# The order in which scores, values and transpositions are written inside the attention units of a hybrid backbone step

## The chip, the cores and the metric

The kernel runs on one core of a Trainium2 chip. The metric is the device time of one execution in microseconds (us); lower is better. The matrix engine (TensorE, PE in the profile) multiplies into PSUM banks; VectorE (DVE), ScalarE (ACT) and GpSimd (POOL) work beside it; SyncE (SP) issues most of the transfers.

## The reference

One layer of a diffusion backbone for 1024 latent tokens and 128 context tokens (1152 in all, D_MODEL 1024): adaLN-modulated RMSNorm, one input projection, a Fourier token mixer and windowed grouped-query attention beside each other, a gated merge, an output projection and a squared-ReLU MLP. What matters here is the attention: 16 query heads in 4 key/value groups, head dimension 64, blocks of 128 queries, a window of 128 tokens to either side, all cached context keys besides, and a learned sink logit per head.

```python
def attend_block(qb, k_all, v_all, sink, mask):
    scores = jnp.einsum('btkgd,blkd->bkgtl', qb, k_all,
                        preferred_element_type=jnp.float32) * (HEAD_DIM ** -0.5)
    if mask is not None:
        scores = jnp.where(mask[None, None, None], scores, NEG_INF)
    sink_col = jnp.broadcast_to(sink.astype(jnp.float32).reshape(N_KV_HEADS, Q_PER_KV)[None, :, :, None, None],
                                scores.shape[:-1] + (1,))
    p = jax.nn.softmax(jnp.concatenate([scores, sink_col], axis=-1), axis=-1)[..., :-1]
    return jnp.einsum('bkgtl,blkd->btkgd', p.astype(v_all.dtype), v_all)
```

The modulation vectors of the layer, `silu(c) @ w_ada + b_ada`, are also computed while attention runs.

## The kernel before, in words

All products are made in float32 precision from a high and a low part of each operand, so an operand x is split into a rounded copy (ScalarE) and the difference (`sub`, L142, VectorE).

The attention stage runs 36 units, one for each pair of key/value group g (0 to 3) and block i of 128 queries (0 to 8; block 8 is the context block). `KWIN` (L43) gives the number nb of 128-key blocks that block i reads: 3 for i = 0 and i = 7, 1 for i = 8, else 4. A unit has up to three kinds of attention steps on TensorE, and each step belongs to a unit of its own age:

- **S**, a score: `score_head(u, h)` (L1008), one for each of the group's four heads of the present unit. Two matmuls (L1024, L1025) into an "s" bank (two of them), one VectorE reduction that adds the mask and takes the maximum (L1026), the exponential on ScalarE (L1038) and, after every second head, a reciprocal on VectorE (L1048) and two multiplications on GpSimd (L1050) that normalise the probabilities "pt".
- **T**, a transposition: `out_t(u, b)` (L1061), one for each key block b of the unit before. Four transposes (L1064) into a "ptp" bank (three of them), the high part "ph" on ScalarE (L1067) and the low part "pl" on VectorE (`sub`, L142).
- **V**, a value step: `out_v(u, b)` (L1071), one for each key block of the unit before that. Two matmuls (L1079, L1080) accumulate in the single "o" bank. After the last block ScalarE copies (L1089) and VectorE adds (L1093, tile "at") the halves, and two stores (L1098) bring the result to `att_d`.

Two more kinds of PE work use the same banks. `put_k` (L1116, called **K** here) transposes key blocks for the scores into a "ptp" bank; `next_keys` (L1361) calls it after the units i = 0, 4 and 7 of a group. `mod_fold` (L272, called **F**, the fold) finishes a block of modulation vectors: one small matmul (L278) into an "s" bank and four small VectorE adds (L282, tile "mods") which free it. It was called once after every unit from s = 3 on, if at least two blocks waited (from s = 30 on, at least one). Ten folds were made in the stage.

The written order of TensorE's instructions holds in this stage (`tc.manual_schedule`, L986); the other engines' queues are ordered by the planner from its own estimate of the time line. Between the steps stand fillers, three matmuls each: pieces of the gate projections, of the next group's queries (whose rotary embedding costs VectorE the pieces L865 to L883) and of the Fourier branch. `unit_order` (L1372) writes the list of a unit's steps with a `None` wherever a filler may go, and the main loop (L1392 to L1408) spreads the fillers of the stage over these places in proportion to the unit's key blocks. After each step `tick` (L899) advances a counter, and work that was put off with `defer` (L893) is issued when the counter reaches it: pl one tick after its transposition, the halves of "o" one to three ticks after the last value step, the rotary pieces one to six ticks after their matmuls.

Before the change an inner unit is written S0 V0 S1 V1 S2 V2 S3 V3 T0 T1 T2 T3, and K and F follow after it.

## Time and profile before

| | us |
|---|---|
| median of 3 runs | 1642.41 |
| lowest and highest of them | 1642.26 and 1643.14 |
| the profiled execution's own time | 1648.12 |
| its span, first to last instruction | 1646.3 |
| mean granted TensorE clock in the span | 0.994 |
| attention scores, first and last start | 272.4 and 679.4 |
| VectorE busy between 270 and 700 us | 305.9 |
| ScalarE busy between 270 and 700 us | 295.4 |

Rows of the timeline read: start, duration, engine, line, operation, result tile and source tiles, shape, count, and in brackets the time that the engine stood idle before and who ended that. Rows of groups read: line, engine, operation, tiles and shapes, count, then busy time and mean ns of one, then idle time before them and what ended it. A matmul's row is longer than its share of the time, because the next one starts while it is still draining: the distance between starts is what counts.

### The profile page before, as it was taken

To read this page: it belongs to the slowest core of one execution; us is meant where nothing else is said; L and a number is where in the kernel's file an instruction comes from. 1 tells how busy PE (TensorE), PEld (TensorE's weight loads), DVE (VectorE), ACT (ScalarE), POOL (GpSimd) and SP (SyncE) were. 2 spreads that over 40 slices of the span, in tenths; PEclk is the share of its full clock that TensorE was granted. 3 is DMA by queue.
4 is the path that set the end of the run, shared out by engine and by line. 5 is a ranking of instruction groups with operands and counts; after the bars stand their busy time and mean duration, and the time that the engine had idled before them with its cause. 6 is when DMAs were issued, how large, how long until landed. Compare 5 with 4: busy or idle time off the path is not lost.

```text
span 1646.3 us, 24742 instructions
## 1 busy us (share of the span) xinstructions
PE 1611.3 (98%) x8361; PEld 1411.8 (86%) x8361; DVE 1129.8 (69%) x2228; ACT 883.1 (54%) x1726; POOL 283.4 (17%) x401
## 2 busy tenths in 40 slices
PE   7999999999999999999999999999999999999998
PEld 5799889899899999889988888888888888888887
DVE  6764266867767865668658767767766588785764
ACT  6753455777687665554446454444444354434542
POOL 1420342445455332310000000000000200000000
PEclk9999999999999999999999999999999999999999
DMA  8352579536444333587585245444445995566741
GB/s 300 124 160 85 176 214 219 148 102 162 126 123 117 103 106 113 169 265 251 162 289 182 103 148 177 156 157 160 163 142 192 347 373 175 191 206 190 254 156 65
DMA packets 216887, 290.19 MB, mean 176 GB/s; under 512 B 27044, under 2 KB 141700, under 8 KB 216632
## 3 DMA queue, kind: packets, MB, share of 16 engines
q1 hardware_dynamic: 205816, 269.73, 51.2%
q0 software_dynamic: 10944, 18.88, 4.1%
q8 instruction: 66, 1.08, 0.3%
q14 instruction: 61, 0.50, 0.1%
HBM read 205.10 MB, written 83.44 MB: 175 GB/s over the span
## 4 chain that ended last, share of the span: by engine, by line
PE 81%; DVE 3%; DMA 1%; ACT 1%; issue 1%; SPq 0%; DVEq 0%; ACTq 0%
PE x L1891 6%; PE x L1892 6%; PE x L1893 6%; PE x L2292 6%; PE x L2293 6%; PE x L2294 6%; PE mm L195 4%; PE mm L197 4%; PE mm L196 4%; PE ptp L1064 3%; PE x L197 2%; PE x L195 2%; PE x L196 2%; PE x L1622 2%; PE x L1624 2%; PE x L1623 2%
## 5 line engine op out<-in xcount | busy, mean ns | idle before, releaser
L142 DVE TENSOR_TENSOR wlo<-wraw,whi 128x1024 fp32r<-128x1024 f32 x96 | 120.2, 1254 | 82.7 <-ACT whi L147 60.2
L1038 ACT ACTIVATE pt<-pt,mx 128x513 f32<-128x513 f32 (+2 forms) x144 | 95.8, 666 | 82.5 <-DVE mx L1026 64.3
L196 PE MATMUL mm<-BR,whi 128*128 128x384 f32 x408 | 137.2, 336 | 0.0
L2293 PE MATMUL x<-BR 128*128 128x512 f32 (+1 forms) x348 | 132.8, 382 | 0.0
L2294 PE MATMUL x<-BR 128*128 128x512 f32 (+1 forms) x348 | 132.2, 382 | 0.0
L195 PE MATMUL mm<-BR,whi 128*128 128x384 f32 x360 | 128.1, 356 | 3.3 <-ACT z L922 2.0
L2292 PE MATMUL x<-BR 128*128 128x512 f32 (+1 forms) x348 | 131.3, 382 | 0.0
L1050 POOL TENSOR_SCALAR pt<-pt,mx 128x512 f32<-128x512 f32 (+2 forms) x144 | 95.3, 675 | 188.6 <-DVE mx L1048 188.2
L1026 DVE CUSTOM_DVE_ANT_0 pt<-s,mask,nsink 128x512 f32<-128x512 f32 (+2 forms) x144 | 96.7, 673 | 40.2 <-PE s L1025 37.9
L197 PE MATMUL mm<-BR,wlo 128*128 128x384 f32 x360 | 121.4, 337 | 0.0
L2265 ACT CAST BR<-aa 128x512 fp32r<-128x512 f32 x80 | 49.7, 622 | 105.8 <-PE x L2293 53.3
L147 ACT CAST whi<-wraw 128x1024 fp32r<-128x1024 f32 x58 | 60.9, 1050 | 84.1 <-DMA wraw<-in_w_ff_dram 39.7
L142 DVE TENSOR_TENSOR pl<-ptp,ph 128x512 fp32r<-128x512 f32 x124 | 83.7, 686 | 23.2 <-ACT ph L1067 22.1
L326 POOL TENSOR_TENSOR macc<-macc,mprod 128x512 f32<-128x512 f32 x70 | 95.1, 1359 | 7.7 <-ACT macc L324 2.5
L196 PEld LDWEIGHTS mm<-BR,whi 128*128 128x128 f32 x408 | 77.2, 189 | 6.1
L1064 PE MATMUL ptp<-ident,pt 128*128 128x128 f32 x496 | 74.3, 273 | 3.6 <-DVE pl L142 3.5
L142 DVE TENSOR_TENSOR BR<-aa,BR 128x512 fp32r<-128x512 f32 x80 | 55.0, 688 | 33.1 <-ACT BR L2265 32.5
L1067 ACT CAST ph<-ptp 128x512 fp32r<-128x512 f32 x124 | 70.7, 586 | 12.2 <-PE ptp L1064 10.8
L195 PE MATMUL mm<-BT,whi 128*128 128x384 f32 x216 | 76.6, 355 | 0.0
L2292 PEld LDWEIGHTS x<-BR 128*128 128x128 f32 x348 | 65.4, 188 | 13.0
L2293 PEld LDWEIGHTS x<-BR 128*128 128x128 f32 x348 | 65.4, 188 | 12.8
L2162 POOL DMA_DIRECT2D BR<-hs_d x4 | 2.1, 535 | 430.9 <-DVE ZR L142 424.4
(495 smaller groups left out, 4846.6 us busy)
## 6 DMA issues: line engine op xcount, KB each, us to landing
aa<-hr_d SPq DMA_DIRECT2D x108, 256.0 KB
ab<-in_w_ff_dram SPq DMA_DIRECT2D x108, 256.0 KB
hr_d<-ZR SPq DMA_DIRECT2D x104, 256.0 KB
wraw<-in_w_in_dram SPq DMA_DIRECT2D x41, 512.0 KB
wraw<-in_w_ff_dram SPq DMA_DIRECT2D x34, 512.0 KB
mraw<-in_w_ada_dram SPq DMA_DIRECT2D x96, 128.0 KB
z_d<-z SPq DMA_DIRECT2D x48, 192.0 KB
q_d<-qt SPq DMA_DIRECT2D x48, 192.0 KB
```

What stands on the lines that cost most here:

```text
L142: return eng.tensor_tensor(dst, raw, hi.bitcast(F32), ALU.subtract)
L195: nc.tensor.matmul(out, ah, bh, start=start, stop=False)
L196: nc.tensor.matmul(out, ah, bl, start=False, stop=False)
L197: return nc.tensor.matmul(out, al, bh, start=False, stop=stop).ins
L1026: nc.vector.tensor_tensor_reduce(out=pt[:, e, :n], in0=sp[:, :n], in1=mask[:, m0 : m0 + n], scale=-0.125, scalar=nsink[:, h0 + e : h0 + e ...
L1064: nc.tensor.transpose(pst[:, h * P : (h + 1) * P], u["pts"][h // 2][:, h % 2, b * P : (b + 1) * P], ident)
L1891: nc.tensor.matmul(po, wh, xh, start=(k == 0 and not cont), stop=False, skip_group_check=cont)
L1892: nc.tensor.matmul(po, wh, xl, start=False, stop=False, skip_group_check=cont)
L1893: nc.tensor.matmul(po, wl, xh, start=False, stop=(k == 3), skip_group_check=cont)
L2292: nc.tensor.matmul(ps, xh, bh, start=start, stop=False, skip_group_check=cont)
L2293: nc.tensor.matmul(ps, xh, bl, start=False, stop=False, skip_group_check=cont)
L2294: nc.tensor.matmul(ps, xl, bh, start=False, stop=stop, skip_group_check=cont)
```

## The change

A string now gives the order of the steps in a unit: S V V V S V S T S T T T. Letters for which a unit has no step left (fewer value steps or fewer transpositions at the ends of a group) are skipped. Three value steps stand between the first and the second score, one transposition stands ahead of the last score, and the fold is written into the unit, behind its second transposition and the filler after that, in place of behind the unit. The fold advances no tick. In a unit that follows a context block there is only one transposition, so no fold is written there; the first fold may come in unit 4 in place of after unit 3, and the last unit is followed by one more.

```diff
@@ -45,6 +45,8 @@
 FILL_0 = 3
 MOD_A = (2, 1)
 PL_LAG = 1
+UNIT = "SVVVSVSTSTTT"
+FOLD_B = 1
 MOD_2 = 2
 MOD_B = 60
 MOD_LATE = 40
@@ -1373,12 +1375,19 @@
             nb = KWIN[prev["i"]][1] if prev else 0
             out = []
             ts = [lambda b=b: out_t(prev, b) for b in range(nb)]
-            for h in range(4):
-                out += [lambda h=h: score_head(u, h), None]
-                if late:
+            b = h = 0
+            for c in UNIT:
+                if c == "S":
+                    out += [lambda h=h: score_head(u, h), None]
+                    h += 1
+                elif c == "V" and late:
                     out += [lambda v=late.pop(0): out_v(*v), None]
-            for f in ts:
-                out += [f, None]
+                elif c == "T" and b < nb:
+                    out += [ts[b], None]
+                    if b == FOLD_B and s > 3:
+                        u["fold"] = lambda: mod_fold(1 if s < 31 else 0, 1)
+                        out.append(u["fold"])
+                    b += 1
             late += [(prev, b) for b in range(nb)]
             return out
 
@@ -1400,12 +1409,13 @@
                     fill_to(base + share * seen / spots)
                 else:
                     f()
-                    tick()
+                    if f is not u.get("fold"):
+                        tick()
             base += share
             next_keys(*units[s])
             pending = u
-            if s > 2:
-                mod_fold(1 if s < 30 else 0, 1)
+            if s == len(units) - 1:
+                mod_fold(0, 1)
         tick(3)
         out_t(pending, 0)
         tick()
```

## The prediction

> **What bounds the kernel now.** I read the page first, then the waits of the matrix engine alone in the attention stage, then a table of windows over that stage, and then the timeline around each kind of wait. The page says who sets the time:

> ```profile
> span 1646.3 us, 24742 instructions
> PE 1611.3 (98%) x8361; PEld 1411.8 (86%) x8361; DVE 1129.8 (69%) x2228; ACT 883.1 (54%) x1726; POOL 283.4 (17%) x401
> ```

> PE is busy 98% of the span, and the change alters no amount of PE work, so it can only win or lose time in which PE stands still or runs slowly. The change lies in the attention units, whose scores start at 272.4 us and end at about 680 us. The view of waits, for PE between 270 and 700 us, is complete in four rows (total, times, longest):

> ```profile
> PE ptp L1064 <- DVE pl L142: 3.5, 4, 2.0
> PE s L1024 <- DVE mods L282: 1.8, 3, 1.1
> PE o L1079 <- DVE at L1093: 1.4, 2, 1.1
> PE o L1080 <- DVE pl L142: 0.6, 1, 0.6
> ```

> That is 3.5 + 1.8 + 1.4 + 0.6 = 7.3 us of visible standstill in ten waits. VectorE ends every one, and the first three kinds are PSUM buffers that come free late. The table of windows adds the clock (eleventh value of a row, after the five busy times):

> ```profile
> 410.00:430.00 20.00, 17.97 (x109) 16.64 (x108) 16.33 (x36) 15.93 (x36) 12.37 (x15) 1.00 0.26 83
> 430.00:450.00 20.00, 20.00 (x107) 18.53 (x106) 15.33 (x37) 12.18 (x27) 5.11 (x9) 0.92 0.57 166
> 610.00:630.00 20.00, 18.92 (x107) 17.36 (x106) 13.11 (x33) 10.59 (x24) 5.89 (x13) 1.00 0.29 79
> ```

> After the longest standstill the granted clock is 0.92 for 20 us, a loss of 20 x 0.08 = 1.6 us; after the waits near 1 us (610 to 630) it stays 1.00. So the prize is at most 7.3 + 1.6 = 8.9 us by these views. A wait also hides a tail, since a 384-column matmul's row is 0.34 us long while the next one starts 0.18 us later (rows below): up to 0.16 us for each of ten waits, 1.6 us more, 10.5 us in all.

> **The pace.** The timeline of PE alone, in the unit with the longest wait:

> ```profile
> 421.79 0.39 PE L1024 MATMUL s<-kth,qT 128*128 128x512 f32 x1
> ...
> 422.77 0.39 PE L1079 MATMUL o<-ph,vg 128*128 128x512 f32 x1
> ...
> 423.41 0.33 PE L196 MATMUL mm<-BT,whi 128*128 128x384 f32 x1
> 423.59 0.34 PE L197 MATMUL mm<-BT,wlo 128*128 128x384 f32 x1
> 423.76 0.60 PE L1064 MATMUL ptp<-ident,pt 128*128 128x128 f32 x4
> ...
> 424.72 0.60 PE L1064 MATMUL ptp<-ident,pt 128*128 128x128 f32 x4
> ...
> 429.37 0.66 PE L1064 MATMUL ptp<-ident,pt 128*128 128x128 f32 x4 [2.03 <-DVE pl L142]
> ```

> Each attention step (score S, value V or transposition T) with its filler takes 0.96 to 0.98 us; I count 0.97. An inner unit has twelve: before, S0 V0 S1 V1 S2 V2 S3 V3 T0 T1 T2 T3, then the fold F; after, S0 V0 V1 V2 S1 V3 S2 T0 S3 T1 F T2 T3. The number of steps and fillers is the same, so throughput costs nothing; the distance in steps between a writer and the next user of its buffer is what changes.

> **Transpositions, 3.5 us.** There are three "ptp" buffers, so T3 waits until T0's low part (pl) is out. That distance was 3 steps, 2.9 us; S3 now stands between, so it is 4, 3.9 us. The VectorE and ScalarE timelines show why 2.9 us did not suffice:

> ```profile
> 425.56 0.56 DVE L866 TENSOR_TENSOR qt<-mm,ropet 128x384 f32<-128x384 f32 x1 [0.87 <-DMA q_d<-qt]
> ...
> 427.09 1.30 DVE L142 TENSOR_TENSOR wlo<-wraw,whi 128x1024 fp32r<-128x1024 f32 x1
> ...
> 428.67 0.65 DVE L142 TENSOR_TENSOR pl<-ptp,ph 128x512 fp32r<-128x512 f32 x1
> ```

> ```profile
> 425.37 1.05 ACT L1291 CAST whi<-wraw 128x1024 fp32r<-128x1024 f32 x1
> 426.44 0.59 ACT L1067 CAST ph<-ptp 128x512 fp32r<-128x512 f32 x1
> ```

> T0's pl ended at 428.67 + 0.65 = 429.3, 5.6 us after T0 began: a weight split and a rotary piece that waited 0.87 us for its transfer lay ahead. One more step leaves 2.0 - 1.0 = 1.0 us of that wait. The other three share 3.5 - 2.0 = 1.5 us; the largest I found is

> ```profile
> 311.05 0.66 PE L1064 MATMUL ptp<-ident,pt 128*128 128x128 f32 x4 [0.83 <-DVE pl L142]
> ```

> and one step of 0.97 us covers each. Gain 3.5 - 1.0 = 2.5 us. Against it: S3's reduction is issued behind T0 and can slip ahead of a late pl. One costs 0.75 us:

> ```profile
> L142 DVE TENSOR_TENSOR pl<-ptp,ph 128x512 fp32r<-128x512 f32 x124 | 83.7, 686 | 23.2 <-ACT ph L1067 22.1
> L1026 DVE CUSTOM_DVE_ANT_0 pt<-s,mask,nsink 128x512 f32<-128x512 f32 x96 | 71.7, 747 | 28.0 <-PE s L1025 26.1 <-POOL pt L1050 0.8 <-issue 0.3
> L282 DVE TENSOR_TENSOR mods<-s,cols 32x4 f32<-32x4 f32 x40 | 6.2, 155 | 0.6 <-PE s L278 0.2
> ```

> So the gain lies between 2.5 - 4 x 0.75 = -0.5 and 3.5 us; I keep 2.5, because in program order T0's pl comes ahead of S3's reduction.

> **The clock, 1.6 us.** A remainder of 1.0 us is like the waits near 1 us at 610 to 630, which left the clock at 1.00, so all 1.6 us come back (bounds 0 and 1.6). [...]

> **The fold, 1.8 us.** The fold takes a score buffer (two exist), and four small VectorE adds release it. It stood after T3, so S1 of the next unit, which gets that buffer, came three places later (F, S0, V0, S1):

> ```profile
> 623.50 0.29 PE L278 MATMUL s<-red,quads 128*128 128x16 f32 x2
> ...
> 624.72 0.39 PE L1079 MATMUL o<-ph,vg 128*128 128x512 f32 x1
> ...
> 626.30 0.51 DVE L282 TENSOR_TENSOR mods<-s,cols 32x4 f32<-32x4 f32 x3
> ...
> 626.95 0.47 PE L1024 MATMUL s<-kth,qT 128*128 128x512 f32 x1 [1.08 <-DVE mods L282]
> ```

> Here the adds ended 626.81 - 623.50 = 3.3 us after F. Now T2 T3 S0 V0 V1 V2 lie between F and S1, 6 x 0.97 = 5.8 us, 2.5 us to spare: gain 1.8 us. What F itself now waits for is S2's reduction, S2 T0 S3 T1 earlier, 3.9 us; before there were six steps. The four adds, 4 x 0.155 = 0.6 us, move ahead of the pl of T2 and T3, which has 5 or 6 steps until its value step.

> **The value accumulator, 1.4 us.** There is one "o" buffer. V0 waits until the last V of the unit before is combined (at):

> ```profile
> 584.35 0.39 PE L1079 MATMUL o<-ph,vg 128*128 128x512 f32 x1
> ...
> 589.24 0.43 DVE L1093 TENSOR_TENSOR at<-o,ot 64x256 f32<-64x256 f32 x1
> ...
> 589.82 0.47 PE L1079 MATMUL o<-ph,vg 128*128 128x512 f32 x1 [1.05 <-DVE at L1093]
> ```

> This is the pair of units at a change of key/value group, where the distance was four steps (S3 T0 S0 V0); it becomes seven (S1 S2 T0 S3 S0 V0 after V2, with V2 itself one place earlier against the scores), some 5.8 us against the 589.67 - 584.35 = 5.3 us that the combination took. Inside a group it goes from six steps to eight. Gain 1.4 us. The stores that follow the combination go out earlier on the sync queue; their reader is the next stage.

> **Value behind transposition, 0.6 us.** After the one-block unit T0 came two steps ahead of its V0 and is now three: gain 0.6 us. In inner units the shortest T-to-V distance stays five (T3 to V3 falls from eight to six, T2 to V2 from seven to five).

> **Probabilities.** T0 now stands one score earlier, so normalisation has less time. The tightest place is a three-block unit followed by S0 V0 S1 S2:

> ```profile
> 377.89 0.34 PE L1024 MATMUL s<-kth,qT 128*128 128x384 f32 x1
> ...
> 385.17 0.39 PE L1024 MATMUL s<-kth,qT 128*128 128x512 f32 x1
> 386.16 0.60 PE L1064 MATMUL ptp<-ident,pt 128*128 128x128 f32 x4
> ```

> ```profile
> 381.38 1.16 POOL L1050 TENSOR_SCALAR pt<-pt,mx 128x384 f32<-128x384 f32 x2
> ```

> GpSimd ended at 382.54; T0 moves from 386.16 to about 385.17. 2.6 us of cover remain, so nothing is charged; if GpSimd ran that much later, all four such places would stall.

> **What is late next.** Three-step distances remain at the key transpositions after units 4 and 7 of a group (T1 to K), six times. VectorE is also denser from S1 to T3: three reductions and four pl, 3 x 0.75 + 4 x 0.69 = 5.0 us, in eight steps, 7.8 us, beside all other work. The nearest row is the 3.5 us that the same three-step distance cost over some 30 units, 0.12 us each: six give 0.7 us; with the adds of a fold ahead in some, I charge 1.0 us (bounds 0, and six times the longest wait seen, 2.0, so 12).

> **Sum.** 2.5 + 1.6 + 1.8 + 1.4 + 0.6 - 1.0 = 6.9 us. Against the profiled execution's own time, 1648.12 us (1.8 of it outside the span), that is 1641.2. The median of the runs is 1642.41, 5.7 us below; I take the same 6.9 us off it: 1635.5 us.

> **The rivals.**
> *The waits move.* If pl is late because of VectorE's queue and not of the distance, the long wait, its clock dip and the other pl waits return, and only 1.8 + 1.4 + 0.6 - 1.0 = 2.8 us are won: 1639.6. For it: pl ended 5.6 us after T0. Against it: only 4 of 124 steps waited. [...] Chance 0.11.
> *The standstill belongs to the profiled execution.* It is 5.7 us longer than the median, and its longest wait has a transfer in it. If these 5.7 us lie in the waits, 6.9 - 5.7 = 1.2 us are left: 1641.2. Chance 0.09.
> *Slower: the rotary pieces collide with the transpositions more often.* Nine such pieces run here,

> ```profile
> L866 DVE TENSOR_TENSOR qt<-mm,ropet 128x384 f32<-128x384 f32 x9 | 4.9, 549 | 0.9 <-DMA q_d<-qt 0.9
> ```

> and VectorE takes its queue in order; one collision cost 2.0 + 1.6 = 3.6 us. Two new ones eat the gain, three give 6.9 - 10.8 = -3.9 us: 1646.3. For it: the planner that orders VectorE's queue sees another PE order and will place everything anew. Against it: one collision in nine before, at a shorter distance. Chance 0.13.

> **How the numbers follow.** The forecast has 0.67. A measurement of this kernel tells about 0.2%, 3.3 us, from no change: faster is the forecast, 0.67; same is the first two rivals, 0.20; slower is the third, 0.13. The range begins at 1642.41 - 10.5 = 1631.9, all standstill gone, and ends at 1644.0, which takes in both middle cases and two to three collisions, and leaves out most of the third rival's 0.13.

> **What would show it.** Right: no wait of a score on "mods" or of V0 on "at"; the wait of "ptp" on pl at or below 1 us in total; a clock of 1.00 in every window of the stage; the last score about 7 us earlier. Wrong: "ptp" waits of the key transposition, transpositions waiting on GpSimd, or a new standstill above 2 us with a clock below 1 behind it. A stage as long as before, with waits gone, would show that the standstill was not the price.

## The result and the profile after

The changed kernel takes 1636.37 us in the median of five runs (1634.74 to 1636.96), the kernel before beside it 1643.14. The ratio, formed over the runs and not the quotient of these two medians (0.9959), is 0.9946 with a 95% interval of 0.9932 to 0.9960. That is faster by about half a per cent, clear of the noise, inside the range and 0.9 us above the forecast. The profiled execution took 1636.59 us, so this time it is no outlier among its runs. Lines below L47 have moved by two (the transposition is now L1066, the score L1026, the value step L1081 and L1082, pl L144, the key transposition L1122). The page:

```profile
span 1634.7 us, 24747 instructions
PE 1606.1 (98%) x8361; PEld 1410.2 (86%) x8361; DVE 1127.0 (69%) x2228; ACT 878.4 (54%) x1726; POOL 280.2 (17%) x401
```

The same number of PE instructions, and 11.6 us less span. The waits of PE between 270 and 700 us:

```profile
PE ptp L1066 <- DVE pl L144: 1.3, 1, 1.3
PE o L1082 <- DVE pl L144: 0.5, 2, 0.3
PE ptp L1122 <- DVE pl L144: 0.4, 1, 0.4
```

Four waits and 2.2 us are left of ten and 7.3. The scores' waits on "mods" and the accumulator's on "at" are gone, and a new row, the key transposition, has come. The windows that show the clock around the longest wait, the last two cut at the edges of the dip (again the eleventh value):

```profile
650.00:670.00 20.00, 18.68 (x98) 15.94 (x97) 14.34 (x34) 10.87 (x30) 8.51 (x17) 0.91 0.37 116
...
660.57:663.98 3.41, 2.08 (x20) 1.97 (x18) 3.41 (x7) 2.01 (x6) 1.55 (x5) 1.00 0.35 96
663.98:667.39 3.41, 3.41 (x10) 2.59 (x10) 1.77 (x5) 0.76 (x3) 0.97 (x2) 0.50 0.79 262
```

The dip is back, behind a wait of 1.3 us: half clock for 3.41 us, so 1.7 us lost. The dip of the kernel before is just as long (429.93 to 433.34, where the window of 20 us had given 1.6). The length of the stage can be read without the waits, from the first score to the first matmul of the next stage's "x" banks. Before, in PE's timeline:

```profile
272.44 0.34 PE L1024 MATMUL s<-kth,qT 128*128 128x384 f32 x1
...
692.59 0.62 PE L1205 MATMUL x<-BR,whi 128*128 128x512 f32 x2
```

And after:

```profile
270.92 0.34 PE L1026 MATMUL s<-kth,qT 128*128 128x384 f32 x1
...
683.11 0.61 PE L1207 MATMUL x<-BR,whi 128*128 128x512 f32 x2
```

420.2 us became 412.2: 8.0 of the 11.6 us lie in the stage, 1.5 ahead of it and 2.1 behind it, where nothing was changed. On either side the profile before has 3.4 us more at half clock (6.8 us instead of 3.4 from 20 us on, and a dip from 914.63 to 918.04 that the profile after has not), which is 1.7 us lost ahead of the stage and 1.7 behind it.

### The profile page after: what moved, and what is told of

It reads as the page before. It is cut to its first block, busy times and chain, and to the rows that moved or that the text cites. A ratio compares the mean times of both kernels' runs of the same rounds, so it can differ in the third digit from the quotient of the medians.

```text
span 1634.7 us, 24747 instructions
## 1 busy us (share of the span) xinstructions
PE 1606.1 (98%) x8361; PEld 1410.2 (86%) x8361; DVE 1127.0 (69%) x2228; ACT 878.4 (54%) x1726; POOL 280.2 (17%) x401
## 3 DMA queue, kind: packets, MB, share of 16 engines
q8 instruction: 66, 1.08, 0.3%
## 4 chain that ended last, share of the span: by engine, by line
PE 81%; DVE 2%; DMA 1%; ACT 1%; issue 1%; POOL 0%; SPq 0%; DVEq 0%; ACTq 0%
PE x L1901 6%; PE x L1902 6%; PE x L1903 6%; PE x L2302 6%; PE x L2303 6%; PE x L2304 6%; PE mm L197 4%; PE mm L199 4%; PE mm L198 4%; PE ptp L1066 3%; PE x L199 2%; PE x L197 2%; PE x L198 2%; PE x L1632 2%; PE x L1634 2%; PE x L1633 2%
## 5 line engine op out<-in xcount | busy, mean ns | idle before, releaser
L144 DVE TENSOR_TENSOR wlo<-wraw,whi 128x1024 fp32r<-128x1024 f32 x96 | 119.8, 1250 | 83.5 <-ACT whi L149 61.0
L197 PE MATMUL mm<-BR,whi 128*128 128x384 f32 x360 | 127.6, 354 | 2.2 <-ACT z L924 1.4
L144 DVE TENSOR_TENSOR pl<-ptp,ph 128x512 fp32r<-128x512 f32 x124 | 83.6, 685 | 19.8 <-ACT ph L1069 19.2
L144 DVE TENSOR_TENSOR BR<-aa,BR 128x512 fp32r<-128x512 f32 x80 | 54.9, 686 | 32.1 <-ACT BR L2275 31.5
L197 PE MATMUL mm<-BT,whi 128*128 128x384 f32 x216 | 76.8, 356 | 0.0
L2302 PEld LDWEIGHTS x<-BR 128*128 128x128 f32 x348 | 65.4, 188 | 13.0
L1066 PE MATMUL ptp<-ident,pt 128*128 128x128 f32 x496 | 75.0, 273 | 1.5 <-DVE pl L144 1.3
L2304 PEld LDWEIGHTS x<-BR 128*128 128x128 f32 x348 | 65.4, 188 | 12.7
L2303 PEld LDWEIGHTS x<-BR 128*128 128x128 f32 x348 | 65.4, 188 | 12.7
```

Source lines behind the costliest of these rows:

```text
L144: return eng.tensor_tensor(dst, raw, hi.bitcast(F32), ALU.subtract)
L197: nc.tensor.matmul(out, ah, bh, start=start, stop=False)
L1066: nc.tensor.transpose(pst[:, h * P : (h + 1) * P], u["pts"][h // 2][:, h % 2, b * P : (b + 1) * P], ident)
L2302: nc.tensor.matmul(ps, xh, bh, start=start, stop=False, skip_group_check=cont)
L2303: nc.tensor.matmul(ps, xh, bl, start=False, stop=False, skip_group_check=cont)
L2304: nc.tensor.matmul(ps, xl, bh, start=False, stop=stop, skip_group_check=cont)
```

## The experiments

The distance theory: the time that the stage loses is set by the number of steps between the writer of a small PSUM buffer and the next user. Its rivals: the fold's place is the whole matter; the planner's chance order of the other queues decides; and, later, the end of the stage decides. All times below are medians beside the kernel before on the same chip; "stage" is the length defined above, in the profiled execution, and "dip" is what of it was lost to half clock there (half of the time spent at 0.50). By the same two measures the kernel before has 420.2 and 1.7, the changed kernel 412.2 and 1.7.

| kernel | us | before | ratio (95% interval) | stage us | dip us |
|---|---|---|---|---|---|
| fold_alone | 1639.76 | 1644.30 | 0.9978 (0.9962 to 0.9994) | 414.6 | 0 |
| order_alone | 1637.74 | 1644.30 | 0.9958 (0.9946 to 0.9970) | 414.4 | 3.4 |
| t_alone | 1639.88 | 1644.30 | 0.9972 (0.9960 to 0.9983) | 413.7 | 0 |
| v_alone | 1640.45 | 1644.30 | 0.9977 (0.9967 to 0.9986) | 415.2 | 0 |
| swap_t | 1640.42 | 1644.45 | 0.9967 (0.9954 to 0.9980) | 415.2 | 3.4 |
| block | 1647.07 | 1644.45 | 1.0016 (1.0004 to 1.0027) | 423.7 | 0 |
| spread | 1641.93 | 1644.45 | 0.9980 (0.9967 to 0.9994) | 414.3 | 0 |
| spread_late | 1643.26 | 1644.45 | 0.9991 (0.9977 to 1.0004) | 418.9 | 5.1 |
| changed_again | 1636.68 | 1644.60 | 0.9956 (0.9940 to 0.9973) | 413.7 | 3.4 |
| tail_old | 1638.83 | 1644.60 | 0.9967 (0.9950 to 0.9984) | 413.7 | 3.4 |
| swap_tail | 1637.05 | 1644.60 | 0.9947 (0.9927 to 0.9967) | 409.2 | 0 |
| spread_tail | 1637.55 | 1644.60 | 0.9956 (0.9941 to 0.9971) | 412.2 | 0 |

Whether a profiled execution had a dip moves its stage by up to 5 us (5.1 in spread_late), so the stages are best compared less the dip: 418.5 us before, and 410.5, 411.0 and 410.3 for the changed kernel, order_alone and changed_again.

**The fold alone.** Edit to the changed kernel:

```diff
-UNIT = "SVVVSVSTSTTT"
+UNIT = "SVSVSVSVTTTT"
```

> The old order of scores, values and transpositions, with only the fold moved behind the second transposition. Distance theory: S1 comes 5 steps (F T2 T3 S0 V0 S1) behind F and no longer 3, so the waits of scores on mods go (1.8 us in the profile of before) and everything else stays, the long ptp wait and the clock dip among it: 1640.5 to 1642 us, 1 to 2.5 us below the kernel before. Rival, that the fold's four adds in the middle of VectorE's queue are the whole matter: all of the change's 6.8 us, 1636.5. Rival, that the planner's new queue order decides and not the distances: anything from 1636 to 1645, with waits of new kinds.

Measured 4.5 us below the kernel before (by the interval 1.0 to 6.2). The waits:

```profile
PE ptp L1066 <- DVE pl L144: 2.7, 4, 1.2
PE o L1081 <- DVE at L1095: 1.4, 2, 1.1
PE o L1082 <- DVE pl L144: 0.6, 1, 0.6
```

The "mods" row is gone, and "at" and the value wait stand as before. That is the distance theory's pattern. The gain is larger than the expected 1 to 2.5 us, and the median lies below the expected range. The long ptp wait was also shorter, 1.2 us in place of 2.0, and no window of the stage fell below a clock of 1.00; neither was expected.

**The order alone.** The fold stands behind the unit as before the change (no unit has a tenth transposition, so none is folded into it):

```diff
-FOLD_B = 1
+FOLD_B = 9
...
-            if s == len(units) - 1:
-                mod_fold(0, 1)
+            if s > 2:
+                mod_fold(1 if s < 30 else 0, 1)
```

> The new order of scores, values and transpositions, with the fold behind the unit as before. Distance theory: V0 V1 V2 now lie between S0 and S1, so S1 is 5 steps behind the fold even where it stood (F S0 V0 V1 V2 S1); the mods waits go without the fold being moved, and the time is that of the changed kernel, 1636 to 1637.5 us. Rival, the fold's place is the matter: 1640 to 1642. Rival, planner's order: anything from 1634 to 1645.

Measured 6.6 us below before, 0.2 us above the expected range, and the waits are those of the changed kernel to 0.1 us:

```profile
PE ptp L1066 <- DVE pl L144: 1.2, 1, 1.2
PE o L1082 <- DVE pl L144: 0.5, 2, 0.3
PE ptp L1122 <- DVE pl L144: 0.4, 1, 0.4
```

No wait on "mods", although the fold was not moved: the three value steps between S0 and S1 are enough. The rival that makes the fold the whole matter falls. What the fold's move adds to the order is not told apart (0.9958 without it, 0.9946 and 0.9956 with it, intervals overlapping).

**The transposition alone.** From here on an edit is the string; this one and the next keep the fold behind the unit.

```diff
-UNIT = "SVVVSVSTSTTT"
+UNIT = "SVSVSVVTSTTT"
```

> Old order but for T0, which stands ahead of S3 (S0 V0 S1 V1 S2 V2 V3 T0 S3 T1 T2 T3); the fold behind the unit as before. Distance theory: T0 to T3 is 4 steps, so the ptp waits fall from 3.5 to about 1 us and the clock dip may go; the waits of scores on mods (1.8) and of V0 on at at the group changes (1.0) stay: 1638.5 to 1641 us, 2 to 4 us below before. Rival, planner's order: no such pattern of waits.

Measured 4.4 us below before. The three largest waits:

```profile
PE ptp L1122 <- DVE pl L144: 2.4, 3, 1.9
PE o L1081 <- ACT pt L1040: 0.7, 1, 0.7
PE s L1026 <- DVE mods L284: 0.5, 1, 0.5
```

The ptp waits of the attention transpositions on pl are gone, as four steps instead of three should make them. But the collision of the kernel before (unit 13, near 427 us) has moved to the key transposition, whose distance is still three steps: 1.9 us there. Two waits that should have stayed did not: "at" is gone and "mods" fell from 1.8 to 0.5 us, although neither distance was changed. Here the distances do not explain all.

**The values alone.**

```diff
-UNIT = "SVVVSVSTSTTT"
+UNIT = "SVVVSVSSTTTT"
```

> Only the values are moved (S0 V0 V1 V2 S1 V3 S2 S3 T0 T1 T2 T3); the fold behind the unit as before. Distance theory: mods waits and at waits go (1.8 and 1.4 us), T0 to T3 stays at 3 steps, so ptp waits of 2.5 to 5 us stay, with a clock dip if one passes 1.3 us: 1638 to 1641 us. Rival, planner's order: no such pattern of waits.

Measured 3.9 us below before:

```profile
PE ptp L1066 <- DVE pl L144: 4.1, 5, 1.8
PE o L1082 <- DVE pl L144: 0.6, 2, 0.3
```

"mods" and "at" gone, ptp still there: the pattern expected. The clock dip expected past 1.3 us did not come: here a wait of 1.8 us left the clock alone.

```profile
640.00:660.00 20.00, 18.17 (x107) 16.68 (x106) 12.23 (x26) 10.70 (x24) 7.86 (x14) 1.00 0.48 168
```

The three parts alone won 4.5, 4.4 and 3.9 us, 12.8 together, where the whole change won 6.8 to 7.9. They do not add up; one reason in the profiles is that none of the three had a dip in the stage and the whole change had one both times.

**All distances short.** The fold stands behind the unit here too.

```diff
-UNIT = "SVVVSVSTSTTT"
+UNIT = "VVVVSSSSTTTT"
```

> All distances that the theory calls dear made short on purpose: V0 V1 V2 V3 S0 S1 S2 S3 T0 T1 T2 T3, the fold behind the unit. S0 to S2 is 2 steps, 1.9 us, and in the kernel before a score's reduction ended 1.5 us after the score began in the middle of 144 cases and 2.5 us or more in one of ten; T0 to T3 is 3 steps. Distance theory: new waits of scores on VectorE's reductions, 5 to 15 us in total, ptp waits of 2.5 to 5 us, no mods and no at waits: 1643 to 1655 us, slower than the change by 7 us at least. Rival, that the distances matter little and the planner fits itself to any order: 1636 to 1642.

Measured 2.6 us above before and some 10 above the change. The waits:

```profile
PE ptp L1066 <- DVE pl L144: 3.4, 4, 1.3
PE s L1026 <- DVE mx L1028: 3.3, 4, 1.2
PE o L1081 <- ACT ph L1069: 1.8, 2, 1.2
PE o L1082 <- DVE pl L144: 1.5, 4, 0.8
```

The score waits on reductions came, with 3.3 us less than the 5 to 15 expected, and so did value waits that were not expected (T0 now lies four steps ahead of V0). The direction is settled: with the same work, shorter distances are slower. The planner did not make up for the order.

**Two steps exchanged.**

```diff
-UNIT = "SVVVSVSTSTTT"
+UNIT = "SVVVSVSTTSTT"
```

> The changed kernel with S3 and T1 exchanged (S V V V S V S T T F S T T, F being the fold). Distance theory: T0 to T3 is still 4 steps and no distance falls below 3, so the time is that of the changed kernel, 1635 to 1638 us, although the planner sees another order and builds other queues. Rival, that the planner's chance order made the gain: a few us off in either direction, 1633 to 1643, with a wait above 1.5 us of a new kind.

A miss: 1640.42, by the medians 4 us slower than the changed kernel, though the intervals of the two ratios overlap. Waits, PE's timeline at the end of the stage, GpSimd's, and the window:

```profile
PE ptp L1066 <- POOL pt L1052: 1.5, 1, 1.5
PE ptp L1066 <- DVE pl L144: 0.7, 1, 0.7
```

```profile
671.56 0.22 PE L1026 MATMUL s<-kth,qT 128*128 128x128 f32 x1
...
674.84 0.33 PE L1066 MATMUL ptp<-ident,pt 128*128 128x128 f32 x1 [1.51 <-POOL pt L1052]
```

```profile
674.41 0.72 POOL L1052 TENSOR_SCALAR pt<-pt,mx 128x128 f32<-128x128 f32 x2 [3.74 <-DVE mx L1050]
```

```profile
670.00:690.00 20.00, 18.36 (x82) 14.39 (x81) 9.33 (x20) 8.38 (x22) 7.31 (x15) 0.83 0.65 208
```

Inside the units nothing got worse: apart from the first row, 1.4 us of waits are left, against 2.2 in the changed kernel. The loss is at the stage's end: the very last transposition needs the probabilities of the last score at 671.56, which GpSimd finished at 674.8. In this order the last score is written one step later, and the clock fell to 0.83 behind that wait (20 x 0.17 = 3.4 us). That is a distance too, one that I had not counted.

**The steps spread evenly, and less so.**

```diff
-UNIT = "SVVVSVSTSTTT"
+UNIT = "SVVSVTSVTSTT"
```

> Steps mixed more evenly: S0 V0 V1 S1 V2 T0 S2 V3 T1 F S3 T2 T3. T0 to T3 is 6 steps (5.8 us) and no longer 4, T1 to the key transposition 4, each score bank 5 or more steps. T0 stands 8 steps, 7.8 us, behind S3 of the unit before, and normalisation ended 3.2 to 7.2 us behind S3 in the kernel before. Distance theory: no ptp waits (2.2 us of the changed kernel's waits go), perhaps one or two transpositions waiting on GpSimd: 1633 to 1636 us. Rival, normalisation is the next bound: transpositions wait on GpSimd in many units, 1638 to 1645 us.

```diff
-UNIT = "SVVVSVSTSTTT"
+UNIT = "SVVSVSTVTSTT"
```

> Between the changed kernel and spread: S0 V0 V1 S1 V2 S2 T0 V3 T1 F S3 T2 T3. T0 to T3 is 5 steps, T0 stands 9 steps behind the unit before's last score. Distance theory: ptp waits below 1 us, nothing on GpSimd: 1633.5 to 1636.5 us. Rival, planner's order: no order between this, spread and the changed kernel.

Both missed: 1641.93 and 1643.26. The rival had part of the first: with T0 eight steps behind the last score, five transpositions waited on GpSimd in spread:

```profile
PE ptp L1066 <- POOL pt L1052: 2.7, 5, 1.0
PE ptp L1122 <- issue: 1.0, 1, 1.0
```

In spread_late the largest wait was again the last transposition's (1.7 us), with a clock of 0.74 from 670 to 690 us. Its profiled execution took 1649.4 us, 6 above its median, so its stage length is not a typical one.

**The end of the stage told apart.** Each of the three kernels below keeps its order up to unit 33 and writes the last two units in the old one; changed_again is the changed kernel once more.

```diff
-            for c in UNIT:
+            for c in UNIT if s < 34 else "SVSVSVSVTTTT":
```

> The changed kernel once more, unaltered, beside the three that follow on one chip: 1635 to 1637.5 us, ratio to the kernel before 0.994 to 0.997.

> The changed kernel with the last two units written in the old order of scores and values (the fold as changed). In the changed kernel's profile the ptp wait of 1.3 us with the clock dip behind it lies in unit 34, and the final transposition starts 2.3 us behind the last score and ends only with its normalisation, 0.7 us lost. Tail theory (the late last score costs at the stage's end): these go, 1633 to 1636 us, 1 to 3 us below the changed kernel. Rival, the wait comes from the Fourier pieces' own work on VectorE there, whatever the order: no difference, 1635.5 to 1637.5.

> swap_t (S3 and T1 exchanged) with the last two units in the old order. Tail theory: swap_t lost 3 to 4 us against the changed kernel because its last score stands one step nearer to the final transposition (1.5 us wait on GpSimd and a clock of 0.83 behind it); with the old tail it comes to 1635 to 1637.5 us, as the distances inside the units say. Rival, planner's chance: it stays at 1639 to 1642.

> spread with the last two units in the old order. Tail theory: most of what spread lost lies at the end, so 1634 to 1638 us. Rival, normalisation is too late in many units (five ptp waits on GpSimd in spread's profile, 2.7 us in all): 1638 to 1643 us, as spread.

changed_again gave 1636.68: the result repeats, 7.9 us below before. swap_tail gave 1637.05 and spread_tail 1637.55, 3.4 and 4.4 us below their versions with the new tail. The intervals overlap a little (0.9954 to 0.9980 against 0.9927 to 0.9967 for swap_t and swap_tail), but in swap_tail's profile the long wait on GpSimd at the end and the clock of 0.83 behind it are gone (spread's own profile had no dip there). So most of what swap_t and spread lost lay in how the last two units are written. Whether it was their distances or the queues that the planner built there, these runs do not tell apart. tail_old missed: 1638.83, no better than the changed kernel. Its waits and those of swap_tail:

```profile
PE ptp L1066 <- DVE pl L144: 1.9, 1, 1.9
```

```profile
PE ptp L1066 <- DVE pl L144: 0.4, 1, 0.4
PE o L1082 <- DVE pl L144: 0.3, 1, 0.3
PE s L1026 <- PE ptp L1066: 0.2, 1, 0.2
```

In tail_old the wait in unit 34 grew from 1.2 to 1.9 us: the old order has three steps from T0 to T3, the changed one four. Less the dip its stage is as long as that of changed_again, 410.3 us, so the earlier last score won nothing there. Yet swap_tail writes the same last two units and waits only 0.4 us there. On VectorE the same two sums of the Fourier weights stand ahead of T0's pl in both. In tail_old the first of them came late:

```profile
660.25 0.69 DVE L1163 TENSOR_TENSOR wraw<-wraw 128x512 f32<-128x512 f32 x1 [1.35 <-POOL pt L1052]
```

VectorE kept to its queue there: it stood idle until 660.25, though ScalarE's copy "ot" for the row of "at" that follows the sum was out at 659.10, and "at" ran at 660.86. In swap_tail the sum did not wait, which is about the difference of 1.5 us. That supports the rival named for tail_old, the Fourier pieces' own work; why GpSimd holds them up in one kernel and not in the other stays open.

swap_tail has the least waiting of all, 0.9 us, and the shortest stage, 409.2 us without a dip, but its ratio of 0.9947 cannot be told from the changed kernel's 0.9946 and 0.9956. No version beat the change measurably.

## Why the prediction was right, and where it was not

**The total.** Forecast 6.9 us off, 6.8 measured by the medians (7.9 in the repetition; the ratio's interval gives 6.6 to 11.2). That it came within 0.1 us is luck: two terms were wrong in opposite directions, as shown below. The visible waits were forecast to fall by 6.3 less the 1.0 charged, 5.3 us; they fell by 7.3 - 2.2 = 5.1.

**The fold and the accumulator** were right: 1.8 and 1.4 us to nothing. order_alone and v_alone show that the values' place alone cures "mods".

**The transpositions.** 1.0 us of wait was to be left; 1.3 was. But it was to be left in unit 13 and came in unit 34. T0 and T3 of that unit in PE's timeline, and VectorE's queue between them:

```profile
657.42 0.60 PE L1066 MATMUL ptp<-ident,pt 128*128 128x128 f32 x4
...
662.58 0.63 PE L1066 MATMUL ptp<-ident,pt 128*128 128x128 f32 x4 [1.32 <-DVE pl L144]
```

```profile
659.60 0.62 DVE L1028 CUSTOM_DVE_ANT_0 pt<-s,mask,nsink 128x384 f32<-128x384 f32 x1
...
660.54 0.69 DVE L1163 TENSOR_TENSOR wraw<-wraw 128x512 f32<-128x512 f32 x1 [0.32 <-POOL pt L1052]
661.15 0.68 DVE L1164 TENSOR_TENSOR wraw<-wraw 128x512 f32<-128x512 f32 x1
661.75 0.68 DVE L144 TENSOR_TENSOR pl<-ptp,ph 128x512 fp32r<-128x512 f32 x1
```

T0's pl ended at 662.4, 5.0 us behind T0, with S3's reduction and two of the Fourier weights' sums ahead of it. The reduction that slips ahead was named as what speaks against the gain, and put aside for the program order; VectorE's queue does not keep that order here.

**The key transposition** was named as what is late next: 1.0 us charged, 0.4 found, and 1.9 in t_alone. **The value steps** were to lose their 0.6 us; that wait went, and two of 0.2 to 0.3 us came in other places: T1 and V1 of a three-block unit lie four short steps apart, and in the one that I followed S0's reduction, itself 1.3 us late behind GpSimd, stood ahead of that pl on VectorE.

**The clock, 1.6 us, is the step that failed.** The dip did not go, it moved to the new longest wait. In the runs, too, the mean granted clock is the same in the median, 0.997 in the 16 runs of the kernel before beside the first experiments and in the five of the change. I took the length of the wait to decide (2.0 us harmful, 1.1 not). But here 1.3 us was followed by half clock, again in changed_again and order_alone (1.2 us, and twice as long a dip, 3.4 us lost), while 1.8 us in v_alone and 1.9 us in t_alone was not.

Length alone does not settle it. Of the stage's waits of 1.2 us and more, seven were followed by half clock (1.2 us in order_alone and in changed_again, 1.3 in the changed kernel, 1.5 in swap_t, 1.7 in spread_late, 1.9 in tail_old, 2.0 in the kernel before) and at least four were not (1.2 us in fold_alone, 1.3 in block, 1.8 in v_alone, 1.9 in t_alone). In the stages of the kernel before and of the changed one the half clock lasted 3.41 us. In the kernel before its dips start at 20.34, 429.93 and 914.63, which is 120 and 142 times 3.413 us apart, and in the changed kernel at 22.27 and 663.98, 188 times; in both the long wait lay whole inside the 3.41 us just ahead of the dip. Two such stretches of the kernel before and two of v_alone:

```profile
426.52:429.93 3.41, 1.38 (x11) 1.06 (x10) 3.41 (x8) 3.36 (x8) 2.38 (x3) 1.00 0.18 53
429.93:433.34 3.41, 3.41 (x13) 3.13 (x13) 2.66 (x5) 1.31 (x3) 0.32 (x2) 0.50 0.76 217
```

```profile
651.79:655.20 3.41, 2.44 (x17) 2.05 (x16) 2.70 (x5) 3.34 (x7) 1.18 (x1) 1.00 0.30 96
655.20:658.61 3.41, 2.55 (x16) 2.46 (x17) 3.15 (x7) 0.59 (x1) 3.25 (x6) 1.00 0.25 76
```

In the kernel before one stretch holds the whole wait of 2.0 us and leaves PE 1.38 us busy; in v_alone, cut at 655.20, the wait of 1.8 us is shared by two, 0.97 and 0.86 us of standstill, and both have a clock of 1.00. That it is the sharing which kept the clock up is my guess: no dip in v_alone's stage shows where such stretches begin there, and no run was made to test it.

**What made up for it** was left at nothing in the sum and stood only in the range: the hidden tails of waits, up to 1.6 us. The stage became 8.0 us shorter with 1.7 us lost to the clock both before and after, so 8.0 us of standstill went, 2.9 more than the view of waits had shown and more than that bound. The bound counted a tail for each of the ten visible waits; a 384-column matmul's row of 0.34 us overlaps the next one, which starts 0.18 us later, and a delay shorter than that overlap does not show as a wait at all. A count of PE's distances between starts in the stage, each less the middle value for matmuls of its shape, says where: those over 0.25 us add up to 9.8 us before and 3.2 after, and the smaller ones fell from 5.6 to 4.3. So the clock term was 1.6 us too large and the hidden standstill, put at nothing in the sum, 2.9 us too small. These are two single executions; the one of the kernel before took 5.0 us more than the median beside the change, and it lost 3.4 us more to dips outside the stage than the one of the change.

**The rivals.** The waits did not stay (5.1 of 7.3 us went). The standstill was not the profiled execution's own: the runs gained as much as the forecast, and what set that execution apart was at least in part dips outside the stage. The rotary pieces were to collide three times for 3.6 us each; no such wait came. Ahead of the key transposition one of them did wait 0.91 us for its transfer again, but it was done 4.7 us before that transposition's pl, which waited for its own high part on ScalarE:

```profile
518.68 0.56 DVE L867 TENSOR_TENSOR qt<-mm,ropet 128x384 f32<-128x384 f32 x1 [0.91 <-DMA q_d<-qt]
...
524.49 1.29 DVE L144 TENSOR_TENSOR pl<-ptp,ph 128x512 fp32r<-128x512 f32 x2 [0.30 <-ACT ph L1069]
```

So the 0.4 us there are not shown to be a collision of that kind. The slower side exists, as block shows, but not here.

## What to carry to other kernels

When an engine is 98% busy and only the order of its work can be changed, count for each small buffer the steps between its writer and its next user, compare them with the time that the evacuation took in its worst row, and lengthen the shortest; then look for the distance that is shortest next, the end of the loop included, where the last item has nothing behind it to hide in. Read a clock dip as a separate term that may return behind a remaining wait (here behind waits of 1.2 and 1.3 us), and don't book it as a gain of removing one; before two profiles are compared, take the time lost to it off both. A view of waits shows only the part of a standstill that outlasts the row of the last matmul (0.34 us for 384 columns here, with starts 0.18 us apart); the length of the stage between two fixed instructions shows all of it.
